# A two-layer hybrid encoder on one core: the gates' logarithm, decays and masks go behind k's convolutions

## The chip, the core and the metric

One NeuronCore of a Trainium2 chip. The metric is the device time of one execution in microseconds (us). The engines are TensorE (PE in the profile), VectorE (DVE), ScalarE (ACT), GpSimd (POOL) and SyncE (SP), each with an instruction stream of its own in a fixed order; they meet only at semaphores. A wait of one instruction therefore holds up everything behind it on its engine.

## The reference

Two pre-norm residual layers over 256 tokens of width 1024, float32 throughout. Each layer projects the normalised input by one weight matrix into eleven parts and runs two token mixers side by side: a gated DeltaNet in both directions (q, k, v through a short convolution and SiLU; 8 heads of 128) and a differential softmax attention (8 heads, 64 wide score halves). What the change touches is the gates of the DeltaNet:

```python
proj = h @ w_in[l]                       # 1024 x 10272
q_a, k_a, v_a, ab_a, z_a, q_b, k_b, v_b, z_b, gate_a, gate_b = split(proj)
qkv = silu(short_conv(concat(q_a, k_a, v_a), conv_w)); q, k = l2norm(q), l2norm(k)
beta = sigmoid(ab[:2])
g = -exp(a_log) * softplus(ab[2:] + dt_bias)          # ab: (4, heads, tokens)
g = cumsum(g)                                         # per chunk
decay = where(lower, exp(g[:, None] - g[None, :]), 0) # per head
L = where(strict, (k * beta) @ k.T * decay, 0); T = inv(I + L)
...                                                   # u, w, state recurrence, both directions
lam = exp(sum(lp[0] * lp[1])) - exp(sum(lp[2] * lp[3])) + lambda_init   # the attention's mixing weight
```

## The kernel before

**Weights.** Every projection streams its weights as tiles of 256 input rows by 512 columns. SP's queue loads `raw` (three buffers), ScalarE rounds it to `hi` (CAST, L308), VectorE forms `lo` = raw - hi (L310), and TensorE multiplies hi by the input's high part, lo by the high part, and hi by the low part. hi and lo have two buffers each, so the cast of a tile starts when TensorE has left the tile two before. Four tiles, kp 0 to 3, make one projection of 512 columns. A few casts are put on VectorE instead (`turned`): q group 1's tile 3, and tiles 0 and 1 of the second qk projection.

**Names.** Tiles carry the layer, the group and the tile in their names: `hi_q011` is layer 0, q group 1, kp 1; `hi_qk0003` is layer 0, qk part 00, kp 3. In the profile the numbers are left out (`hi_q`, `hi_qk`).

**One layer, in program order around the change.** First half of v for the attention; convolutions of k (two groups: projection `pf_k`, then ScalarE `cvk` and tanh `thk`, VectorE the taps, TensorE's transposes `ctk`, ScalarE's sums of squares `sqj` into `ssk`); second half of v (`vb1`); then

- `log_decays` (from L726): from the k sums of squares `kss` the norm `nrm` (a power on POOL, L730) and their logarithm; the softplus of the gates, `Ln` of `e_`/`ev` (both lie in one tile `ge`, which the logarithm reads together with kss, 128x80, L732); `glog`, TensorE's cumulative sums `grps`, their copy `grow`, which POOL's queue writes to DRAM (`gdr`), TensorE's transposes `gcps`, `ngc`, `E_` and `nE`, and the exponents' biases `lnc`.
- `conv("q", …, 0)` (`pf_q`) and `qk_part(0, 0)` (`pp_qk`, with a copy `stg`, rope on VectorE in tiles `r`, and TensorE's transposes `qkt`, copied to `qkT`).
- four times `decays(g, c)` and `weigh_k(g, c)`: a broadcast of gdr to all partitions into `B` (0.5 MB, POOL's queue), `kds`, two masks by `affine_select` on POOL, eight exponents (ScalarE, L791), then on VectorE `dsum` and `A` = kk * dsum with TensorE's gram matrix `kk`. The third and fourth broadcast are held behind the second mask (`cut`).
- `turn_blocks`, `conv("q", …, 1)`, `qk_part(0, 1)`, the convolutions of v, and later the gate parts (`zb`, `za`, …) among which the attention's scores `sc` run.

**What sets the order.** The code's order is a wish: a list scheduler places every instruction on its engine by what it expects to be ready, with the weights at high priority; `with behind(ins)` keeps an instruction from being placed before `ins`, and `mark[...]` holds such instructions (`mark["k01", 1][0]` is the cast of layer 0, k group 1, tile 1). What it gives out is the fixed order of each engine. Both layers are built by the same code.

## Time and profile before

| what | value |
|---|---|
| median of 3 runs | 751.38 us (750.87 to 751.71) |
| the profiled execution | 750.2 us, span 748.5 us |
| mean granted TensorE clock | 0.997 |
| busy: PE, DVE, ACT, POOL | 739.9, 588.6, 475.3, 143.5 us |
| TensorE in layer 0: both k groups, second half of v | 24.8 to 48.6, 48.7 to 60.2 us |
| then q group 0, qk part 00, q group 1, qk part 01 | 60.2 to 72.7, 72.7 to 87.0, 87.0 to 99.5, 99.5 to 112.6 us |
| the 32 exponents of layer 0 | 91.5 to 103.5 us |

A row of a timeline gives the start in us, the duration, the engine, the line, the operation with what it writes and reads, and how many of a kind follow one another; in brackets stands how long the engine was idle before it, and what ended that. Matrix multiplies are pipelined, so their cadence is read from one start to the next, not from the duration. Layer 1 repeats every row some 366 us later.

### The profile page before, as it was taken

The page shows a single profiled execution, that of the slowest core. Times are in us where ns is not written, and L with a number is a line of the kernel's source. Part 1 is how long each engine was busy: PE and PEld are TensorE (multiplying, and loading weights), DVE is VectorE, ACT ScalarE, POOL GpSimd, SP SyncE. Part 2 cuts the span into 40 slices and gives each one's busy share as a digit, 9 for nine tenths or more (in the row PEclk, how much of TensorE's full clock was granted, in tenths as well). Part 3 has the DMA queues.
Part 4 walks back from the last instruction along what each step waited for, and adds up shares of the span by engine and source line. Part 5 has one row for each costly group of instructions (what it writes and reads, how often), then busy time and mean ns, then how long its engine had stood idle before and what let it go on. Part 6 is the DMA issues. An engine that isn't in the chain of part 4 may idle for free.

```text
span 748.5 us, 13886 instructions
## 1 busy us (share of the span) xinstructions
PE 739.9 (99%) x5164; PEld 640.8 (86%) x5164; DVE 588.6 (79%) x1109; ACT 475.3 (64%) x1016; POOL 143.5 (19%) x221
## 2 busy tenths in 40 slices
PE   8999999999999999999999999999999999999996
PEld 6999889977888889888889889889778888998885
DVE  8686899999985965578667779999999679537782
ACT  6657675667876576645454677655687758566552
POOL 6000441112022450000000025202110425301000
PEclk9999999999999999999999999999999999999999
DMA  8752767776667462567674358768666747335641
GB/s 261 235 171 80 214 206 214 209 213 194 208 185 178 146 183 83 171 200 248 199 232 141 85 144 257 217 183 228 198 172 195 198 135 231 92 114 202 219 142 56
DMA packets 73733, 135.45 MB, mean 181 GB/s; under 512 B 12944, under 2 KB 13921, under 8 KB 73666
## 3 DMA queue, kind: packets, MB, share of 16 engines
q1 hardware_dynamic: 64750, 113.65, 50.0%
q0 software_dynamic: 7936, 19.35, 9.0%
q10 hardware_dynamic: 980, 1.58, 0.6%
q8 instruction: 40, 0.66, 0.4%
q14 instruction: 27, 0.22, 0.1%
HBM read 125.53 MB, written 9.01 MB: 180 GB/s over the span
## 4 chain that ended last, share of the span: by engine, by line
PE 97%; DMA 1%; issue 1%; DVE 0%; ACT 0%; SPq 0%; POOLq 0%; POOL 0%; DVEq 0%; ACTq 0%
PE pp_vb L369 4%; PE pp_qk L325 4%; PE pp_qk L324 4%; PE pp_qk L326 4%; PE sc L1033 2%; PE pp_o L369 2%; PE pp_za L325 2%; PE pf_v L385 2%; PE pf_k L385 2%; PE pf_v L389 2%; PE pp_gb L324 2%; PE pp_gb L325 2%; PE pp_zb L324 2%; PE pf_k L387 2%; PE pf_k L389 2%; PE pf_q L387 2%
## 5 line engine op out<-in xcount | busy, mean ns | idle before, releaser
L325 PE MATMUL pp_qk<-lo_qk,hT 128*128 128x512 f32 x128 | 50.7, 396 | 0.0
L326 PE MATMUL pp_qk<-hi_qk,hT 128*128 128x512 f32 x128 | 50.0, 390 | 0.0
L310 DVE TENSOR_TENSOR lo_qk<-raw_qk,hi_qk 128x1024 fp32r<-128x1024 f32 x32 | 39.5, 1234 | 9.6 <-ACT hi_qk L308 9.1
L324 PE MATMUL pp_qk<-hi_qk,hT 128*128 128x512 f32 x128 | 45.2, 394 | 0.0
L308 ACT CAST hi_qk<-raw_qk 128x1024 fp32r<-128x1024 f32 x28 | 29.4, 1049 | 23.6 <-PE pp_qk L326 11.8
L1043 ACT ACTIVATE es<-sc,mx 128x256 f32<-128x256 f32 x64 | 29.6, 474 | 19.6 <-DVE mx L1041 19.6
L310 DVE TENSOR_TENSOR lo_pb<-raw_pb,hi_pb 128x1024 fp32r<-128x1024 f32 x16 | 19.6, 1225 | 21.5 <-ACT hi_pb L308 21.2
L387 PE MATMUL pf_q<-hT,hi_q 128*128 128x256 f32 x128 | 36.2, 286 | 0.0
L385 PE MATMUL pf_q<-hT,hi_q 128*128 128x256 f32 x128 | 36.1, 286 | 0.0
L385 PE MATMUL pf_v<-hT,hi_v 128*128 128x256 f32 x128 | 35.8, 285 | 0.0
L385 PE MATMUL pf_k<-hT,hi_k 128*128 128x256 f32 x128 | 35.8, 285 | 0.0
L387 PE MATMUL pf_v<-hT,hi_v 128*128 128x256 f32 x128 | 35.8, 284 | 0.0
L387 PE MATMUL pf_k<-hT,hi_k 128*128 128x256 f32 x128 | 35.6, 283 | 0.0
L389 PE MATMUL pf_q<-hT,lo_q 128*128 128x256 f32 x128 | 34.8, 285 | 0.0
L389 PE MATMUL pf_v<-hT,lo_v 128*128 128x256 f32 x128 | 34.5, 287 | 0.0
L389 PE MATMUL pf_k<-hT,lo_k 128*128 128x256 f32 x128 | 34.3, 283 | 0.0
L670 DVE SCALAR_TENSOR_TENSOR cvq<-pf_q,cw,cvq 128x254 f32<-128x254 f32 (+1 forms) x64 | 29.9, 476 | 1.9 <-ACT cvq L666 1.4
L308 ACT CAST hi_pa<-raw_pa 128x1024 fp32r<-128x1024 f32 x16 | 16.9, 1054 | 22.2 <-PE pp_pa L326 16.0
L670 DVE SCALAR_TENSOR_TENSOR cvk<-pf_k,cw,cvk 128x254 f32<-128x254 f32 (+1 forms) x64 | 28.5, 478 | 2.1 <-ACT cvk L666 1.4
L670 DVE SCALAR_TENSOR_TENSOR cvv<-pf_v,cw,cvv 128x254 f32<-128x254 f32 (+1 forms) x64 | 29.7, 475 | 0.1
L325 PEld LDWEIGHTS pp_qk<-lo_qk,hT 128*128 128x128 f32 x128 | 24.0, 188 | 6.1 <-DVE lo_qk L310 1.3
L310 DVE TENSOR_TENSOR lo_pa<-raw_pa,hi_pa 128x1024 fp32r<-128x1024 f32 x16 | 19.6, 1224 | 11.2 <-ACT hi_pa L308 11.2
(409 smaller groups left out, 2541.2 us busy)
## 6 DMA issues: line engine op xcount, KB each, us to landing
raw_qk<-in_w_in_dram SPq DMA_DIRECT2D x32, 512.0 KB, 4.0
raw_k<-in_w_in_dram SPq DMA_DIRECT2D x16, 512.0 KB, 4.4
raw_q<-in_w_in_dram SPq DMA_DIRECT2D x16, 512.0 KB, 3.8
raw_v<-in_w_in_dram SPq DMA_DIRECT2D x16, 512.0 KB, 3.8
raw_zb<-in_w_in_dram SPq DMA_DIRECT2D x16, 512.0 KB, 3.9
raw_za<-in_w_in_dram SPq DMA_DIRECT2D x16, 512.0 KB, 3.8
raw_ga<-in_w_in_dram SPq DMA_DIRECT2D x16, 512.0 KB, 4.8
raw_pb<-in_w_pb_dram SPq DMA_DIRECT2D x16, 512.0 KB, 3.8
```

The lines of the kernel that those rows point to most:

```text
L308: high = (V.tensor_copy if kp in turned else S.copy)(hi[:, :, :n], raw[:, :, :n]).ins
L310: mark[nm, kp] = high, V.tensor_tensor(lo[:, :, :n], raw[:, :, :n], hi[:, :, :n].bitcast(F32), ALU.subtract).ins
L324: T.matmul(o, act[kt // 4][:, 0, kt % 4, ts_], hi, start=kt == 0, stop=False)
L325: T.matmul(o, act[kt // 4][:, 0, kt % 4, ts_], lo, start=False, stop=False)
L326: mark["proj"] = T.matmul(o, act[kt // 4][:, 1, kt % 4, ts_], hi, start=False, stop=kt == KT - 1).ins
L369: mark["proj"] = T.matmul(o, act[kt // 4][:, pa, kt % 4, ts_], ws[kt][1 + pw], start=kt == 0 and n_ == 0, stop=kt == KT - 1 and n_ == 2).ins
L385: T.matmul(o, hi[:, cs], act[kt // 4][:, 0, kt % 4, :], start=first, stop=False, skip_group_check=True)
L387: T.matmul(o, hi[:, cs], act[kt // 4][:, 1, kt % 4, :], start=False, stop=False, skip_group_check=True)
L389: T.matmul(o, lo[:, cs], act[kt // 4][:, 0, kt % 4, :], start=False, stop=done, skip_group_check=True)
L670: V.scalar_tensor_tensor(ca[:, o0:o1], acc[:, b, o0 + sft : o1 + sft], cw[:, j, cb : cb + 1], ca[:, o0:o1], ALU.mult, ALU.add)
L1033: mm = T.matmul(sp[n][:, qt * SEQ : (qt + 1) * SEQ], qkT[h // 4][rows, 0, h % 4, qt * P : (qt + 1) * P], qkT[h // 4][rows, 1, h % 4, :], s ...
L1043: S.activation(es[:, n, qt, :], spv[:, qt, :], AF.Exp, bias=mx[:, n, qt : qt + 1], accum_out=s_all[:, h, n, qt : qt + 1])
```

## The change

`log_decays` is split. `gates()` is called after the code of k's convolutions; its logarithm of the gates alone (128x64) is held behind the cast of k group 1, tile 0, and what follows from it (glog, grps, grow, gdr, gcps, ngc, E, nE) may be placed from there on. `lambdas()` takes the exponential of the attention's mixing weight, held behind the cast of k group 1, tile 1. `spread()` issues all four broadcasts in a row on POOL's queue, then the eight masks; the hold by `cut` goes. `log_decays` keeps the k norms, their logarithm (128x16) and the biases; `decays` keeps kds and the exponents.

```diff
         ls = small.tile([P, 2], F32, tag="ls", name=f"ls{l}")
         V.tensor_reduce(ls, lq, AX.X, ALU.add)
-        S.activation(ls, ls, AF.Exp)
         neglam = small.tile([P, 1], F32, tag="neglam", name=f"neglam{l}")
-        V.scalar_tensor_tensor(neglam, ls[:, 1:2], -lam0, ls[:, 0:1], ALU.add, ALU.subtract)
...
+        ngc = small.tile([P, 4, NH], F32, tag="ngc", name=f"ngc{l}")
...
         def log_decays():
...
-            S.activation(e_, e_, AF.Ln)
-            V.scalar_tensor_tensor(ev, a_, 0.0, ev, ALU.max, ALU.add)
-
+            S.activation(kss, kss, AF.Ln)
             for d in range(2):
                 V.scalar_tensor_tensor(lnc[:, d], ev[:, :, d * 8 : d * 8 + 8], -1.0, kss,
                                        ALU.mult, ALU.subtract)
+            V.tensor_tensor(lnc.rearrange("p d c h -> p (d c) h"), lnc.rearrange("p d c h -> p (d c) h"),
+                            ngc, ALU.add)
+
+        def lambdas():
+            with behind(mark[f"k{l}1", 1][0]):
+                S.activation(ls, ls, AF.Exp)
+            V.scalar_tensor_tensor(neglam, ls[:, 1:2], -lam0, ls[:, 0:1], ALU.add, ALU.subtract)
+
+        def gates():
+            with behind(mark[f"k{l}1", 0][0]):
+                S.activation(ev, ev, AF.Ln)
+            V.scalar_tensor_tensor(ev, a_, 0.0, ev, ALU.max, ALU.add)
             glog = small.tile([P, NM, 16], F32, tag="glog", name=f"glog{l}")
...
-        def decays(g, c, after=None):
+        def spread():
+            for g in range(2):
+                for c in range(NM):
+                    hs4 = slice(4 * g, 4 * g + 4)
+                    G.dma_start(out=B[:, c, hs4].rearrange("p h d i -> p (h d i)"),
+                                in_=gdr[c, hs4].rearrange("h d i -> (h d i)").partition_broadcast(P))
+            for g in range(2):
+                for c in range(NM):
+                    dec = B[:, c, 4 * g : 4 * g + 4].rearrange("p h d i -> p d h i")
+                    for d in range(2):
+                        sg = 1 - 2 * d
+                        G.affine_select(
+                            out=dec[:, d], in_=dec[:, d], compare_op=ALU.is_ge, fill=BIG,
+                            base=0, pattern=[[0, 4], [sg, P]], channel_multiplier=-sg)
+
+        def decays(g, c):
...
-            with behind(after):
-                G.dma_start(out=B[:, c, hs4].rearrange("p h d i -> p (h d i)"),
-                            in_=gdr[c, hs4].rearrange("h d i -> (h d i)").partition_broadcast(P))
...
-                mark["cut"] = G.affine_select(
...
         conv("k", C_KA, 0, 1)
+        gates()
         for _ in proj_by_tile(hT, wl, C_VB + 512, evac_v(1), f"vb{l}1", places2, spare=range(4),
...
+        lambdas()
+        spread()
         log_decays()
...
-        cut = mark["cut"]
         decays(0, 1)
...
-        decays(1, 0, cut)
+        decays(1, 0)
...
-        decays(1, 1, cut)
+        decays(1, 1)
```

Three places of the order in layer 0 matter for the prediction; layer 1 has the same rows with its own numbers. First ScalarE. Before, from the cast of q group 1's first tile on (`hi_q010`), `E_` being the exponential of ngc and `thq`, `cvq` the convolution's tanh and first tap:

```order
L308 CAST hi_q010_1196<-raw_q010_1198 128x1024
L676 ACTIVATE thq000_961<-cvq001_964 128x256
L757 ACTIVATE E_0_364<-ngc0_828 128x32
L586 COPY stg0000_1063<-pp_qk0000_989 128x512
L676 ACTIVATE thq002_978<-cvq002_972 128x256
L666 ACTIVATE cvq003_981<-pf_q001_834,cw0_294 128x256
L308 CAST hi_q011_1226<-raw_q011_1228 128x1024
L586 COPY stg0001_1076<-pp_qk0001_990 128x512
L308 CAST hi_q012_1256<-raw_q012_1258 128x1024
L599 ACTIVATE qkT0_0_307<-qkt0000_1070 128x4x128
L791 ACTIVATE B0_366<-B0_366,lnc0_362 128x128 x4
```

Now, from the cast of the last tile of qk part 00 on (the exponents are the rows of L805):

```order
L308 CAST hi_qk0003_1074<-raw_qk0003_1076 128x1024
L805 ACTIVATE B0_365<-B0_365,lnc0_360 128x128
L674 ACTIVATE thq000_990<-cvq001_993 128x256
L805 ACTIVATE B0_365<-B0_365,lnc0_360 128x128 x7
L308 CAST hi_q010_1197<-raw_q010_1199 128x1024
L805 ACTIVATE B0_365<-B0_365,lnc0_360 128x128 x3
L674 ACTIVATE thq002_1007<-cvq002_1001 128x256
L805 ACTIVATE B0_365<-B0_365,lnc0_360 128x128 x5
L664 ACTIVATE cvq003_1010<-pf_q001_863,cw0_294 128x256
L805 ACTIVATE B0_365<-B0_365,lnc0_360 128x128 x2
L586 COPY stg0000_1092<-pp_qk0000_1018 128x512
L805 ACTIVATE B0_365<-B0_365,lnc0_360 128x128
```

The next row is the cast of `hi_q011`, and twelve more exponents stand before that of `hi_q012`. All 32 were behind the last ScalarE cast of q group 1; 31 of them are ahead of it now.

VectorE, q group 1's last three tiles. Before:

```order
L310 TENSOR_TENSOR lo_q011_1227<-raw_q011_1228,hi_q011_1226 128x1024
L591 TENSOR_TENSOR r40001_1078<-stg0001_1076,sincos_284 128x128
L670 SCALAR_TENSOR_TENSOR cvq003_981<-pf_q001_834,cw0_294,cvq003_981 128x255
L592 TENSOR_TENSOR r40001_1078<-stg0001_1076,sincos_284 128x128
L670 SCALAR_TENSOR_TENSOR cvq003_981<-pf_q001_834,cw0_294,cvq003_981 128x254
L593 TENSOR_TENSOR stg0001_1076<-r40001_1078 128x8x8
L594 TENSOR_TENSOR stg0001_1076<-r40001_1078 128x8x8
L310 TENSOR_TENSOR lo_q012_1257<-raw_q012_1258,hi_q012_1256 128x1024
L308 CAST hi_q013_1286<-raw_q013_1288 128x1024
```

Now:

```order
L310 TENSOR_TENSOR lo_q011_1228<-raw_q011_1229,hi_q011_1227 128x1024
L812 TENSOR_TENSOR A0_364<-kk001_1146,dsum001_1144 128x512
L668 SCALAR_TENSOR_TENSOR cvq003_1010<-pf_q001_863,cw0_294,cvq003_1010 128x254
L591 TENSOR_TENSOR r40001_1107<-stg0001_1105,sincos_284 128x128
L592 TENSOR_TENSOR r40001_1107<-stg0001_1105,sincos_284 128x128
L811 TENSOR_TENSOR dsum010_1161<-B0_365 128x512
L593 TENSOR_TENSOR stg0001_1105<-r40001_1107 128x8x8
L594 TENSOR_TENSOR stg0001_1105<-r40001_1107 128x8x8
L812 TENSOR_TENSOR A0_364<-kk010_1163,dsum010_1161 128x512
L308 CAST hi_q013_1287<-raw_q013_1289 128x1024
L310 TENSOR_TENSOR lo_q012_1258<-raw_q012_1259,hi_q012_1257 128x1024
```

The dsum and A steps have come in, and the VectorE cast of tile 3 (`hi_q013`) stands ahead of tile 2's lo (`lo_q012`), where it stood behind it.

TensorE, at the second block of scores, in the gate projection zb. Before:

```order
L326 MATMUL pp_zb001_2022<-hi_zb003_2077,hT0_1_127 128x512
L1033 MATMUL sc011_2121<-qkT0_0_307 128x256
L1033 MATMUL sc010_2120<-qkT0_0_307 128x256
L1033 MATMUL sc011_2121<-qkT0_0_307 128x256
L1033 MATMUL sc010_2120<-qkT0_0_307 128x256
L324 MATMUL pp_zb010_2164<-hi_zb010_2166,hT0_0_126 128x512
```

Now:

```order
L326 MATMUL pp_zb001_2023<-hi_zb003_2078,hT0_1_127 128x512
L1047 MATMUL sc011_2122<-qkT0_0_307 128x256
L597 MATMUL qkt0111_2006<-ident_81,stg0111_1999 128x128 x4
L1047 MATMUL sc010_2121<-qkT0_0_307 128x256
L1047 MATMUL sc011_2122<-qkT0_0_307 128x256
L1047 MATMUL sc010_2121<-qkT0_0_307 128x256
L324 MATMUL pp_zb010_2165<-hi_zb010_2167,hT0_0_126 128x512
```

Four transposes qkt, which stood some ten rows ahead, have come between the first score multiply and the other three. Each of these rows is two instructions in the profile.

More of the change, by code (lines that the diff above doesn't have):

```diff
@@ L754, in log_decays @@
                 T.transpose(gc_ps[:, dc * 8 : dc * 8 + 8], grow[:, dc, :], ident[:8, :8])
-            ngc = small.tile([P, 4, NH], F32, tag="ngc", name=f"ngc{l}")
             V.tensor_scalar(ngc, gc_ps[:, :32].rearrange("p (c h) -> p c h", c=4), -1.0, None, ALU.mult)
@@ L758, in log_decays @@
             V.tensor_scalar(nE, E_, -1.0, None, ALU.mult)
-            V.tensor_tensor(lnc.rearrange("p d c h -> p (d c) h"), lnc.rearrange("p d c h -> p (d c) h"),
-                            ngc, ALU.add)
         A = big.tile([P, 2, NM, 4, P], F32, tag="A", name=f"A{l}")
@@ L784, in decays @@
             for d in range(2):
-                sg = 1 - 2 * d
-                mark["cut"] = G.affine_select(
-                    out=dec[:, d], in_=dec[:, d], compare_op=ALU.is_ge, fill=BIG,
-                    base=0, pattern=[[0, 4], [sg, P]], channel_multiplier=-sg).ins
                 for j4 in range(4):
```

## The prediction

> **What bounds the kernel now.** I read the head of the page first, then the chain that ended last, then TensorE's waits, and only then the stretches around the change.
>
> ```profile
> span 748.5 us, 13886 instructions
> PE 739.9 (99%) x5164; PEld 640.8 (86%) x5164; DVE 588.6 (79%) x1109; ACT 475.3 (64%) x1016; POOL 143.5 (19%) x221
> PE 97%; DMA 1%; issue 1%; DVE 0%; ACT 0%; SPq 0%; POOLq 0%; POOL 0%; DVEq 0%; ACTq 0%
> PE idle L410 <- DVE ones L407: 1.1, 1, 1.1
> PE pp_vb L454 <- ACT hT L234: 0.4, 1, 0.4
> PE pp_vb L454 <- DVE hT L238: 0.3, 1, 0.3
> ```
>
> TensorE is busy 99% of the span and is 97% of the chain; the last three rows are all its waits, 1.8 us (line, releaser, total, times, longest), and all lie at a layer's start, far from this change. The change removes no matrix multiply, so what it can win is only small hesitations of TensorE that the wait view does not list. What it can lose is open: any weight tile that arrives late stops TensorE.
>
> Where it acts is the stretch of q's convolutions and the first qk projection, 66 to 105 us in layer 0 and about 366 us later again in layer 1.
>
> ```profile
> 81.00:87.00 6.00, 6.00 (x38) 5.01 (x36) 5.31 (x14) 2.74 (x7) 2.02 (x4) 1.00 0.61 155
> 87.00:93.00 6.00, 6.00 (x53) 6.00 (x52) 5.42 (x13) 4.37 (x11) 3.57 (x6) 1.00 0.90 294
> 93.00:99.00 6.00, 6.00 (x52) 6.00 (x52) 5.48 (x7) 5.36 (x18) 3.27 (x7) 1.00 0.93 311
> ```
>
> Columns: stretch, length, then busy time of PE, PEld, DVE, ACT and POOL, granted clock, DMA share, GB/s. TensorE is full at clock 1.00 and VectorE at 5.3 to 5.5 of 6; ScalarE has 2.74 of 6 before 87 and 5.36 after 93. The 32 exponents of the decays are what fills it after 93. Where exactly they stand among the weight casts is the question of this prediction.
>
> ```profile
> 86.22 0.42 ACT L676 ACTIVATE thq<-cvq 128x256 f32<-128x256 f32 x1
> 86.54 0.47 ACT L666 ACTIVATE cvq<-pf_q,cw 128x256 f32<-128x256 f32 x1
> 86.90 1.04 ACT L308 CAST hi_q<-raw_q 128x1024 fp32r<-128x1024 f32 x1
> 87.83 0.60 ACT L586 COPY stg<-pp_qk 128x512 f32<-128x512 f32 x1
> 97.85 2.45 ACT L791 ACTIVATE B<-B,lnc 128x128 f32<-128x128 f32 x8 [0.62 <-POOL B L786]
> 88.29 1.22 DVE L310 TENSOR_TENSOR lo_q<-raw_q,hi_q 128x1024 fp32r<-128x1024 f32 x1
> 93.38 1.47 DVE L308 CAST hi_q<-raw_q 128x1024 fp32r<-128x1024 f32 x1 [0.92 <-PE pf_q L387]
> 97.56 0.80 DVE L308 CAST hi_qk<-raw_qk 128x1024 fp32r<-128x1024 f32 x1
> ```
>
> A weight tile goes raw (DMA), hi (a cast, mostly on ScalarE), lo (raw minus hi on VectorE, 1.22 us), TensorE. hi and lo have two buffers each, so a cast starts only when TensorE has left the tile two before. Now the second cast of q1 (86.90) follows short work, its lo ends at 89.51 and TensorE reads it first at 90.22 (row below): 0.7 us of slack, and that is all the chain has. The exponents come late, where the fourth q1 tile and the first two of the next projection are cast on VectorE instead (93.38), so no weight waits behind them.
>
> **The change, part by part.** I write R for the time at which TensorE leaves the second tile of the first qk projection, which releases the ScalarE cast of the fourth.
>
> ```profile
> 86.22 1.05 PE L772 MATMUL kk<-kq 128*128 128x128 f32 x8
> 87.03 0.36 PE L385 MATMUL pf_q<-hT,hi_q 128*128 128x256 f32 x1
> 89.87 0.60 PE L597 MATMUL qkt<-ident,stg 128*128 128x128 f32 x4
> 90.22 0.36 PE L389 MATMUL pf_q<-hT,lo_q 128*128 128x256 f32 x1
> 106.77 0.62 PE L324 MATMUL pp_qk<-hi_qk,hT 128*128 128x512 f32 x2
> 109.49 0.61 PE L324 MATMUL pp_qk<-hi_qk,hT 128*128 128x512 f32 x2
> 112.62 0.38 PE L385 MATMUL pf_v<-hT,hi_v 128*128 128x256 f32 x1
> ```
>
> 1. *The exponents among q1's casts (ScalarE).* In the new order eight exponents and a tanh stand between the cast of the last qk tile and that of q1's first, and eleven exponents with a tanh, a cvq and a stg copy between q1's first and second. By the starts in the rows a cast takes 0.93 (86.90 to 87.83), tanh 0.32, cvq 0.36; neighbours overlap by about 0.1, so a stg copy takes some 0.48 of its 0.60 and eight exponents 2.36 of their 2.45, 0.295 each. ScalarE then starts the second q1 cast at R + 0.2 (release) + 0.93 + 2.36 + 0.32 + 0.93 + 3.25 + 0.32 + 0.36 + 0.48 = R + 9.2. It ends 1.04 later; lo follows at once or after the rope steps of the stg copy that now stand ahead of it on VectorE (0.5 later), and takes 1.22: R + 11.4 to R + 12.0. TensorE wants it after two qk tiles (2.72 each, 106.77 to 109.49), q1's first tile (24 steps of 0.12: 23 stand between 87.03 and 89.87), the kk block now ahead of it (86.22 to 87.03 and the switch, 0.9), four hi rows (0.48) and qkt (0.35): R + 10.1 to 10.3. So it waits 1.1 to 1.8 us; I take 1.4. This holds if each exponent finds its data, which the POOL rows below bear out.
>
> 2. *q1's third tile (VectorE).* Its lo now stands behind the VectorE cast of the fourth tile, in the order before ahead of it. That cast waits for TensorE to leave the second tile, then takes 1.47 (93.38), then lo 1.22, 2.7 us after the release, where TensorE needs it after kk 0.9, qkt 0.35 and four hi rows 0.48, that is 1.73 after: 0.95 late, less if the cast takes the 0.8 us it took at 97.56. I take 0.7 (0 to 0.95). Terms 1 and 2 come in both layers, since the order is the same in both.
>
> 3. *A score block cut in two (TensorE).*
>
> ```profile
> 165.09 1.14 PE L1033 MATMUL sc<-qkT 64*128 64x256 f32 x8
> ```
>
> Eight score instructions of half height, alternating between the two halves, take 1.14 us, 0.28 a pair. If the halves of a pair run side by side, the lone ones that the cut leaves on each side cost a pair's time each, about 0.4 us with the switch; if not, only the switch of 0.1. 0 to 0.5, I take 0.4.
>
> 4. *Two table loads more per layer, around k's convolutions (ScalarE).*
>
> ```profile
> L732 ACT ACT_TABLE_LOAD  x2: 1283/1283/1283, 73.8 to 439.7; - x2
> L732 ACT ACTIVATE ge<-ge x2: 270/270/270, 75.1 to 441.0; 128x80 f32<-128x80 f32 x2
> 36.50 0.48 ACT L666 ACTIVATE cvk<-pf_k,cw 128x256 f32<-128x256 f32 x1 [1.25 <-PE pf_k L389]
> 39.92 1.05 ACT L308 CAST hi_k<-raw_k 128x1024 fp32r<-128x1024 f32 x1 [0.88 <-PE pf_k L387]
> 41.19 1.22 DVE L310 TENSOR_TENSOR lo_k<-raw_k,hi_k 128x1024 fp32r<-128x1024 f32 x1
> 43.20 0.28 PE L389 MATMUL pf_k<-hT,lo_k 128*128 128x256 f32 x1
> 402.29 0.47 ACT L666 ACTIVATE cvk<-pf_k,cw 128x256 f32<-128x256 f32 x1 [1.19 <-PE pf_k L389]
> 405.77 1.05 ACT L308 CAST hi_k<-raw_k 128x1024 fp32r<-128x1024 f32 x1 [1.83 <-PE pf_k L387]
> ```
>
> 2 x 1.28 plus at most 0.27 for each of the two short functions behind them. In layer 0 they fill the idle 1.25 ahead of 36.50 and the 0.88 ahead of the cast at 39.92, which comes 0.5 to 0.9 later; lo_k ended at 42.41 and was read at 43.20, so 0.79 covers it but for 0.1 at worst. In layer 1 the idle 1.19 and 1.83 of the last two rows cover it. I take 0 (0 to 0.3 a layer); if the cover goes, each tenth is a tenth of the time. The Trainium skill (ScalarE: Activation LUTs, "What ACT_TABLE_LOAD costs") puts a drain of about 1380 ns on top of each load, 2.66 us in all: by it the cast would be 2.8 us later still and TensorE would stall some 2.6 us here. The trace does not show that drain: the first load starts at 73.8 and the logarithm behind it at 75.1, so the row's 1.28 decides.
>
> 5. *What goes from the q stage.* The logarithm there shrinks from 128x80 to 128x16 (0.27 us) between its two loads, which stay; glog, grow, ngc, E and nE leave VectorE and ScalarE ahead of q1, under 2 us of off-path work. 0. The grps, gcps and four kk blocks are moved on TensorE, the same in number and in switches: 0, but R, 78.2 before (grps follows it), comes behind grps (0.97), gcps (0.4) and two kk now, at about 81.3. With the exponents done earlier, A and the blocks behind it come sooner; the hesitations in the tile from 109.49 to 112.62, 3.13 against 2.72, may go. 0 to 0.4, I take 0.2 off.
>
> 6. *Broadcasts and masks (POOL and its queue).*
>
> ```profile
> 72.66 0.63 PE L324 MATMUL pp_qk<-hi_qk,hT 128*128 128x512 f32 x2
> 78.22 1.04 PE L745 MATMUL grps<-tri,glog 128*8 128x128 f32 x8
> 89.43 0.34 POOL L783 TENSOR_TENSOR kds<-B,lnc 128x4 f32<-128x4 f32 x1 [4.58 <-DMA B<-gdr]
> L786 POOL TENSOR_SCALAR_AFFINE_SELECT B<-B x8: 627/862/1536, 89.7 to 101.0; 128x512 f32<-128x512 f32 x8
> DMA to landing us min/median/max: 5.6/6.7/7.5
> raw_q<-in_w_in_dram SPq DMA_DIRECT2D x1, 512.0 KB, 7.5
> raw_q<-in_w_in_dram SPq DMA_DIRECT2D x16, 512.0 KB, 3.8
> ```
>
> The grps block now stands 44 steps of 0.12 ahead of q0's end (72.66), so at about 67.3, 11 us ahead of its old place. The first broadcast was used 11.2 us behind it (78.22 to 89.43), so the first is to be had at 78.5, and the others, at 5.6 to 7.5 us to landing and more when four share the engines, by 85. Eight masks of 0.86 are done by 87, the last two 1.7 us behind the last landing. ScalarE reaches the first exponents at 82.4 and the ninth, which needs the third broadcast, at 86 (from R = 81.3). So they are ready: 0, with 0 to 1.4 us as the upper bound if the third is late. SP's queue keeps its order. Its loads took 7.5 us beside broadcasts against 3.8 in the middle case, and still came in time (the cast at 93.38 waited 0.92 us for TensorE, not for its load); the broadcasts only collide with other loads now.
>
> Sum per layer: 1.4 + 0.7 + 0.4 + 0 - 0.2 = 2.3 us, twice 4.6. The profiled execution took 750.2 us, its span 748.5, 1.2 under the median of the runs, 751.38; the difference is added to the median: **756.0 us**. With each term at its ends the forecast goes from 2 x 0.7 to 2 x 3.5: 752.8 to 758.4.
>
> **The rivals.** 0.2% is 1.5 us, about what a measurement here can tell from no change; all chances are counted by it.
>
> *The stall is absorbed* (same). If ScalarE's chain is shorter than I add up, or TensorE reaches q1 a microsecond later than I place it, the 0.7 us of slack holds and only the cut block is left, or not even that: 750.9 to 752.5. For it: a shift of 1.5 us in either term is enough, and I add up ten durations. Against: 19 exponents of 0.295 are 5.6 us set before a cast that had 0.7 to spare. 25%.
>
> *Faster.* The mechanism is the early end of the decays: A is done before the next projection, and TensorE loses its hesitations there and at the block's start. It is worth 0.4 us in each of the few places, at most 1.7 us in both layers, so 749.7; it decides only if terms 1 to 3 are all nought. 5%.
>
> *The four broadcasts crowd the weights* (slower still). Their 2 MB in one go against a load of 0.5 MB per 2.72 us: at the 311 GB/s of the row at 93, an even split leaves the weights 155 of the 193 they need, and over some 13 us they fall behind by 0.5 MB, about 1.6 us at that rate, against about 1 us of slack. With the third broadcast late too it adds 1 to 2 us a layer: 758 to 760. The Trainium skill (DMA: Bandwidth & Descriptors, "Queues, rings and completion order") has each engine alternate between queues packet by packet, which is the even split; the 7.5 us above agrees with it. Against: two pairs of broadcasts ran nearly back to back before and cost nothing. 10%.
>
> *The table loads stop k's convolutions* (slower too). If a load holds ScalarE a microsecond longer than its row, the cast of k's third tile comes 2 us later in layer 0 and 0.8 - 0.9 - 2 leaves TensorE 2.1 us short: 758.1. Against: the logarithm's start, right behind its load. 3%.
>
> **How the numbers follow.** Forecast (752.9 to 758.4) 57%, crowding 10%, table loads 3%, same 25%, faster 5%. Slower is 70%. The range runs from 751.0, which leaves out the faster case and about half of the same, to 759.6, which leaves out the end of the crowding. The likeliest case's own range is 752.9 to 758.4.
>
> **What would show it.** Step 1: TensorE rows waiting for ScalarE's hi_q or VectorE's lo_q at about 91 to 93 us (457 to 459), the second q1 cast with 11 exponents ahead. Step 2: a second wait at 95 to 98, on lo_q. Step 3: the second score block at about 1.5 us with qkt inside, not 1.07. Step 4: no wait on lo_k near 43. Step 6: the masks done by 87, POOL not named in ScalarE's waits. The prediction is wrong if q1's tiles follow at 2.88 plus kk and qkt with no wait, or if the long wait stands at k's convolutions instead.

## The result, and the profile after

| | before | after |
|---|---|---|
| median of 4 runs | 751.12 us (750.83 to 751.71) | 758.96 us (758.79 to 760.65) |
| ratio | | 1.0108, 95% interval 1.0091 to 1.0126 |
| span of the profiled execution | 748.5 us | 757.0 us |

The change made the kernel 7.8 us slower; the forecast was 756.0. One execution of the kernel before, beside e1 to e4, took 820.42 us at a mean granted clock of 0.85; it is in no ratio and no spread below. The same lines of the page as before:

```profile
span 757.0 us, 13901 instructions
PE 742.7 (98%) x5164; PEld 641.7 (85%) x5164; DVE 587.5 (78%) x1109; ACT 481.8 (64%) x1022; POOL 142.2 (19%) x221
PE 90%; ACT 3%; DVE 3%; DMA 2%; issue 2%; POOL 0%; POOLq 0%; DVEq 0%; SPq 0%; ACTq 0%
```

No engine has notably more work. What is new is in the chain, where ScalarE, VectorE and the DMA queues now hold 8%, and in TensorE's waits:

```profile
PE pf_q L385 <- ACT stg L586: 2.7, 2, 1.4
PE pp_qk L325 <- DVE lo_qk L310: 1.5, 3, 0.7
PE pf_q L389 <- DVE lo_q L310: 0.8, 1, 0.8
PE pf_q L385 <- ACT hi_q L308: 0.2, 1, 0.2
```

None of these four was there before, and all lie in the first qk projection and in q group 1. The stretches of layer 0 that the prediction showed, now:

```profile
81.00:87.00 6.00, 5.11 (x22) 3.60 (x21) 5.57 (x10) 4.46 (x11) 6.00 (x9) 1.00 0.75 272
87.00:93.00 6.00, 4.64 (x32) 4.08 (x31) 4.88 (x10) 6.00 (x18) 0.30 (x2) 1.00 0.55 174
93.00:99.00 6.00, 6.00 (x53) 5.93 (x52) 6.00 (x14) 6.00 (x19) 0.00 (x0) 1.00 0.33 91
```

ScalarE is full from 87 to 99, where q1's second and third casts stand. TensorE is short of 6.00 in the first half of that stretch and in the 6 us before it. To see where the time went, I compared the start of every projection on TensorE in the two traces, and, inside a projection, each step from one matrix multiply to the next with its usual step:

| place | layer 0 | layer 1 | what the steps show |
|---|---|---|---|
| q group 0 and first qk projection | +1.5 | +1.5 | waits of 0.85 and 0.36 us on lo_qk (layer 1: 0.80, and 0.23 for q1's first tile) |
| q group 1 and second qk projection | +1.7 | +2.6 | 1.5 in the middle of q1's first tile, 0.3 at the lo of its third; in layer 1 also 0.9 at the start of its first; 0.5 less at the end |
| from there to the layer's end | +0.8 | +0.8 | the score block cut in two |

With 0.25 us less at the start, these make the 8.5 us between the spans, up to rounding. The waits named in a row do not add up to all of it; the rest lies in smaller steps, which I have not followed. Now the rows. The long wait, on ScalarE and TensorE, layer 0 and in the last row layer 1:

```profile
83.89 0.42 ACT L674 ACTIVATE thq<-cvq 128x256 f32<-128x256 f32 x1 [0.96 <-DVE cvq L668]
...
86.26 1.03 ACT L308 CAST hi_q<-raw_q 128x1024 fp32r<-128x1024 f32 x1
...
90.80 0.56 ACT L586 COPY stg<-pp_qk 128x512 f32<-128x512 f32 x1
...
91.57 1.03 ACT L308 CAST hi_q<-raw_q 128x1024 fp32r<-128x1024 f32 x1
91.41 0.38 PE L385 MATMUL pf_q<-hT,hi_q 128*128 128x256 f32 x1 [1.36 <-ACT stg L586]
462.11 0.39 PE L385 MATMUL pf_q<-hT,hi_q 128*128 128x256 f32 x1 [1.35 <-ACT stg L586]
```

The step at 91.41 is the thirteenth of q1's first tile, the first that writes q1's second accumulator. Its weights and activations were read before; what it waits for is the accumulator's PSUM bank, which the stg copy at 90.80 sets free by reading the finished qk product out, and that copy stands behind ten exponents since the cast at 86.26. The cast at 91.57 is that of q1's second tile, 5.3 us behind the first with eleven exponents between. It comes late too, as VectorE and TensorE show:

```profile
93.40 1.22 DVE L310 TENSOR_TENSOR lo_q<-raw_q,hi_q 128x1024 fp32r<-128x1024 f32 x1
94.67 0.39 PE L389 MATMUL pf_q<-hT,lo_q 128*128 128x256 f32 x1
```

This lo ends at 94.62 and is read at 94.67, with no slack. Without the 1.36 us at the bank TensorE would have been there at 93.3 and waited for the lo instead, by an estimate from these rows 1.3 us: one group of exponents makes two things late, and only the first of them shows as a wait. Layer 1 has the same pair (lo ends at 465.31, read at 465.38).

In the kernel before, both had time to spare. The same copy and the first read of the second tile's lo there:

```profile
85.74 0.59 ACT L586 COPY stg<-pp_qk 128x512 f32<-128x512 f32 x1 [2.02 <-PE pp_qk L326]
90.90 0.28 PE L389 MATMUL pf_q<-hT,lo_q 128*128 128x256 f32 x1
```

The copy ended at 86.33 and the thirteenth step came at 88.55, 2.2 us later. The lo ended at 89.51 and was first read at 90.90, 1.4 us later: a tile has 24 steps, so the row at 90.22 from which the prediction took 0.7 us is the last step of q1's first tile and reads that tile's lo.

q1's third tile on VectorE and TensorE, now:

```profile
98.00 1.22 DVE L310 TENSOR_TENSOR lo_q<-raw_q,hi_q 128x1024 fp32r<-128x1024 f32 x1
99.27 0.39 PE L389 MATMUL pf_q<-hT,lo_q 128*128 128x256 f32 x1
```

The lo ends at 99.22, and the step that reads it comes 0.41 us behind the one before it (98.86) instead of 0.12. Layer 1 has the same 0.3 at 469.97. The first qk projection, third tile, layer 0; the first row is of the kernel before:

```profile
75.61 1.06 ACT L308 CAST hi_qk<-raw_qk 128x1024 fp32r<-128x1024 f32 x1 [0.20 <-PE pp_qk L326]
...
77.52 1.28 ACT L674 ACT_TABLE_LOAD   x1 [0.77 <-DVE cvq L668]
79.50 1.04 ACT L308 CAST hi_qk<-raw_qk 128x1024 fp32r<-128x1024 f32 x1
79.27 0.90 DVE L679 SCALAR_TENSOR_TENSOR kq<-thq,cvq 128x256 f32<-128x256 f32 x1 [1.72 <-ACT thq L674]
80.99 1.62 DVE L310 TENSOR_TENSOR lo_qk<-raw_qk,hi_qk 128x1024 fp32r<-128x1024 f32 x1
82.67 0.50 PE L325 MATMUL pp_qk<-lo_qk,hT 128*128 128x512 f32 x1 [0.69 <-DVE lo_qk L310]
```

The cast stands behind a table load and a tanh that wait for VectorE's taps; before, it stood ahead of them (75.61). And VectorE's steps are stretched: kq takes 0.90 and lo 1.62, against 0.42 and 1.22. In layer 1 the third tile is in time. There the fourth tile's lo is late, which stands behind five taps on VectorE (451.51 to 453.59) and takes 1.68 us, and TensorE waits 0.8 us for it; and the load of q1's first tile is late as well (the last two rows are of the DMA view: KB, and us to landing, of that load now and of the same load before):

```profile
453.59 1.68 DVE L310 TENSOR_TENSOR lo_qk<-raw_qk,hi_qk 128x1024 fp32r<-128x1024 f32 x1
456.94 1.05 ACT L308 CAST hi_q<-raw_q 128x1024 fp32r<-128x1024 f32 x1 [1.46 <-DMA raw_q<-in_w_in_dram]
459.30 0.39 PE L389 MATMUL pf_q<-hT,lo_q 128*128 128x256 f32 x1 [0.76 <-DVE lo_q L310]
raw_q<-in_w_in_dram SPq DMA_DIRECT2D x1, 512.0 KB, 10.5
raw_q<-in_w_in_dram SPq DMA_DIRECT2D x1, 512.0 KB, 3.7
```

Last the cut block of scores, with the four transposes inside:

```profile
175.20 0.70 PE L1047 MATMUL sc<-qkT 64*128 64x256 f32 x2
175.82 0.66 PE L597 MATMUL qkt<-ident,stg 128*128 128x128 f32 x4
176.41 1.13 PE L1047 MATMUL sc<-qkT 64*128 64x256 f32 x6
177.47 0.73 PE L324 MATMUL pp_zb<-hi_zb,hT 128*128 128x512 f32 x2
```

2.27 us from 175.20 to 177.47. Before, the whole block took 1.06 and the transposes inside the projection 0.44, so the cut costs 0.77.

### The profile page after: what moved, and what is told of

It is laid out like the page before. It is cut to its first block, busy times and chain, and to the rows that moved or that the text cites. A ratio compares the mean times of both kernels' runs of the same rounds, so it can differ in the third digit from the quotient of the medians.

```text
span 757.0 us, 13901 instructions
## 1 busy us (share of the span) xinstructions
PE 742.7 (98%) x5164; PEld 641.7 (85%) x5164; DVE 587.5 (78%) x1109; ACT 481.8 (64%) x1022; POOL 142.2 (19%) x221
## 4 chain that ended last, share of the span: by engine, by line
PE 90%; ACT 3%; DVE 3%; DMA 2%; issue 2%; POOL 0%; POOLq 0%; DVEq 0%; SPq 0%; ACTq 0%
PE pp_vb L369 4%; PE pp_qk L325 3%; PE pp_qk L326 3%; PE pp_qk L324 3%; PE sc L1047 2%; PE pp_o L369 2%; PE pp_zb L324 2%; PE pf_k L385 2%; PE pf_v L389 2%; PE pp_gb L325 2%; PE pp_za L325 2%; PE pp_gb L324 2%; PE pf_v L385 2%; PE pp_za L324 2%; PE pf_k L389 2%; PE pf_k L387 2%
```

## The experiments

Theory: the early gates let the exponents, and in the first qk projection a table load with a tanh, come ahead of weight casts on ScalarE; TensorE waits for those casts and for the stg copy among them. Rival: the four broadcasts and eight masks in a row crowd the DMA engines and VectorE. Each kernel was timed in five rounds beside the kernel before on the same chip; ratios are to that kernel, and 0.1% is 0.75 us. The kernel as changed stands at 1.0108.

**e1, the score block whole.**

```diff
-                    with behind(None if qt or not n else after), tc.high_priority(offset=HP):
+                    with behind(None if qt or not n else after), \
+                         behind(mark["qkt"] if h == 1 and n and not qt else None), tc.high_priority(offset=HP):
```

(`mark["qkt"]` is the last transpose of the qk projections.)

> The changed kernel with one edit: the second score block's first multiply is held behind the transposes qkt that had come between its multiplies, so the block runs whole; the order differs from the changed kernel in that row alone, once per layer. The trace of the changed kernel has the cut block with qkt inside at 2.27 us, against 1.06 for a whole block and 0.44 for qkt inside a projection, so the cut costs 0.8 us a layer. Theory (the time lies in TensorE's stream: cut block and late casts): 1.6 us less than the changed kernel, 757.3. Rival (the cut is only a place where a wait shows that would come later anyway, the score chain being set by VectorE and ScalarE): no gain, 758.9.

Measured 756.90 us, ratio 1.0088 (1.0075 to 1.0100): 0.2% less than as changed, 1.5 us, as the rows say, though the two intervals overlap. The trace is clearer: the block takes 1.06 us again (174.97 to 176.03), and from v's convolution to the layer's end TensorE falls back by 0.1 us instead of 0.8. The block was a loss by itself.

**e2, the exponents behind q1's casts.** The four `decays` and `weigh_k` calls go behind `conv("q", C_QA, 1, 1)`, and

```diff
-                    S.activation(dec[:, d, j4, :], dec[:, d, j4, :], AF.Exp,
-                                 bias=lnc[:, d, c, h : h + 1])
+                    with behind(mark[f"q{l}1", 2][0]):
+                        S.activation(dec[:, d, j4, :], dec[:, d, j4, :], AF.Exp,
+                                     bias=lnc[:, d, c, h : h + 1])
```

> The changed kernel with the code of the decays put behind that of q group 1's convolution and the 32 exponents held behind the cast of q1's third tile (kp 2). Gates, broadcasts, masks and table loads stay as in the changed kernel; the score block comes out whole again. Theory (exponents among ScalarE's weight casts stop TensorE in q1): the waits in q1 go, 1.7 and 2.6 us, and the cut block's 0.8 twice, while the waits on lo_qk in the first qk projection, 1.2 to 1.5 us a layer, stay, since the cast of its third tile still stands behind a table load and a tanh: 752.8 to 754.2. Rival (four broadcasts and eight masks in a row crowd DMA and VectorE): q1 stays slow, 757 or more.

Measured 753.66 us, ratio 1.0045 (1.0028 to 1.0061): more than half of the loss is gone, with gates, broadcasts, masks and loads as in the change. The wait on the stg copy in q1 is gone in its trace; what is left stands in the first qk projection, as expected, and at q1's first tile in layer 1, which waited 3.17 us for its raw load on ScalarE:

```profile
PE pp_qk L325 <- DVE lo_qk L310: 1.6, 3, 1.2
78.80 1.49 DVE L679 SCALAR_TENSOR_TENSOR kq<-thq,cvq 128x256 f32<-128x256 f32 x1 [1.73 <-ACT thq L674]
```

**e3, broadcasts and masks as before.** `spread()` goes; each `decays` has its broadcast and masks again, and `cut` its hold.

```diff
-        spread()
...
-        decays(1, 0)
+        decays(1, 0, cut)
```

> The changed kernel without the broadcasts and masks in a row: each decay issues its own broadcast and masks again, the later two held by cut as before; gates and table loads stay early. The exponents still stand among the weight casts, 16 of them ahead of q1's first cast and the first 4 ahead of the fourth qk tile's. Theory (order of ScalarE): still slow, 757 to 762, with longer waits at q1's first tile. Rival (broadcasts and masks in a row): back to 751 to 753.

Measured 758.89 us, ratio 1.0103 (1.0090 to 1.0116): the whole loss is still there. TensorE now waits longest on lo in q1:

```profile
PE pf_q L389 <- DVE lo_q L310: 3.1, 3, 1.5
```

So the loss does not need the row of broadcasts and masks. Since the exponents stand still earlier here than in the change, the run does not show that the row costs nothing.

**e4, the gates in their old place.** One logarithm again, and `gates()` called from `log_decays`; `spread()` behind it.

```diff
-        gates()
         for _ in proj_by_tile(hT, wl, C_VB + 512, evac_v(1), f"vb{l}1", places2, spare=range(4),
...
-            S.activation(kss, kss, AF.Ln)
+            S.activation(e_, e_, AF.Ln)
+            gates()
...
-            with behind(mark[f"k{l}1", 0][0]):
-                S.activation(ev, ev, AF.Ln)
```

> The changed kernel with the gates' part back in its old place behind the k norms, one logarithm for both; broadcasts and masks stay in a row, the table load for the mixing weight stays early. TensorE's, ScalarE's and VectorE's orders come out nearly as before the change, with the exponents behind q1's casts. Theory (the early gates let the exponents come among the casts, and that is the loss): 751 to 752. Rival (broadcasts and masks in a row): half or more of the loss stays, 755 to 759.

Measured 752.28 us, ratio 1.0013 (1.0004 to 1.0022). Seven of the eight microseconds come back; the early gates are the cause, through the order that they allow. The one that stays is, by its trace, the rival's, and it has a row: the fourth q1 tile's cast, which VectorE does, waited for its load, and the load took 10.5 us beside four broadcasts in a row.

```profile
95.34 0.76 DVE L308 CAST hi_q<-raw_q 128x1024 fp32r<-128x1024 f32 x1 [2.31 <-DMA raw_q<-in_w_in_dram]
```

**f1 and g1, the table loads behind the cast (on e2).**

```diff
-            S.activation(kss, kss, AF.Ln)
+            with behind(mark[f"qk{l}00", 2][0]):
+                S.activation(kss, kss, AF.Ln)
...
-        log_decays()
         conv("q", C_QA, 1, 0)
         qk_part(0, 0)
+        log_decays()
```

> On top of the kernel with the exponents late (e2): the code of the k norms is put behind that of the first qk projection and their logarithm is held behind the cast of its third tile (kp 2), so this cast no longer stands behind two table loads; TensorE's and POOL's orders are those of e2. In e2 TensorE still waited on lo_qk: 1.37 and 0.35 us in layer 0, 0.26, 0.36, 0.20 and 0.93 in layer 1. Theory A (the cast is late by its place on ScalarE): most of these 3.5 us go, 750.5 to 751.8. Theory B (POOL's masks, which run at 79 to 87 us, stretch VectorE's steps, kq 1.49 us instead of 0.42 and lo_qk 1.55 instead of 1.22): the masks stay where they are, so the waits stay for the most part, 752.8 to 754.

> The same kernel as f1 once more, for its spread: f1's executions went from 751.35 us (the profiled one, with 0.72 us of waits in layer 0's q1 and 1.4 in layer 1's, clock 1.00 throughout) to 756.63. Theory (TensorE's granted clock halves for some microseconds behind waits in q1, as the profiles of f3 at 90 to 94 and 458 to 464 us show it, in some executions and not in others): times from 751 to 757 again, and where the profile has a stretch below 1.00 near 88 to 96 or 456 to 466 its time is 1.5 to 3 us higher than 751.4 for each. Rival (weight loads beside the four broadcasts are late in some executions): a slow profile shows waits on DMA or on casts that wait for DMA, at clock 1.00.

Measured 754.36 us, ratio 1.0049 (1.0032 to 1.0066), and again 754.04, 1.0039 (1.0026 to 1.0053): by their medians no better than e2, so theory A's forecast of the time failed; but the fourteen executions go from 751.35 to 756.63. The profiled ones are among the lowest, 751.35 and 752.45. In them the waits of the first qk projection are gone from layer 0 and 0.3 in layer 1, although the masks run beside VectorE as before (lo_qk took 1.72 us): theory A holds for those waits. What is left there are 0.7 us in layer 0 and some 1 to 1.7 in layer 1 at q1's first two tiles, where the first cast waits for its load (0.7 to 2.5 us on ScalarE). Neither profiled execution shows why others of the same kernel take 3 to 5 us more.

**f2, the masks behind the last lo (on e2).**

```diff
+        def masks():
+            late = small.tile([P, 1], F32, tag="late", name=f"late{l}")
+            slow = G.tensor_copy(late, mark["lo", f"qk{l}00", 3][:, 0, 0:1].bitcast(F32)).ins
+            ...                                      # the eight masks, each behind(slow)
...
         qk_part(0, 0)
+        masks()
```

> On top of the kernel with the exponents late (e2): POOL first copies one column of the fourth qk tile's lo and only then runs the eight masks, so they start behind VectorE's last lo of that projection; ScalarE's order there, with the cast behind the loads, is that of e2. Theory A (place of the cast): 753 to 754 as e2. Theory B (masks stretch VectorE): kq back to 0.42 and lo_qk to 1.22, that is 1.4 us earlier, most of the waits in the first qk projection go, 751.3 to 752.5; the masks then run beside q1's lo steps, which may cost some tenths there, since the slack was 0.7.

Measured 755.18 us, ratio 1.0055 (1.0043 to 1.0067). The half of theory B on VectorE is shown, the forecast of the time is not. VectorE and POOL in layer 0:

```profile
79.69 0.42 DVE L680 SCALAR_TENSOR_TENSOR kq<-thq,cvq 128x256 f32<-128x256 f32 x1 [1.72 <-ACT thq L675]
80.99 1.23 DVE L311 TENSOR_TENSOR lo_qk<-raw_qk,hi_qk 128x1024 fp32r<-128x1024 f32 x1
91.19 1.67 DVE L311 TENSOR_TENSOR lo_q<-raw_q,hi_q 128x1024 fp32r<-128x1024 f32 x1
85.77 6.01 POOL L799 TENSOR_SCALAR_AFFINE_SELECT B<-B 128x512 f32<-128x512 f32 x8
```

With the masks out of the way kq is back at 0.42 and lo_qk at 1.23, and the wait of 1.37 us at the third qk tile is gone, with the cast where it was. But the masks now lie on q1, where lo_q takes 1.67 instead of 1.22 and TensorE waits 1.1 us in layer 0. In layer 1 it waits 2.1 at q1's first tile, whose cast stood idle 3.97 us for its load. The wait at the third qk tile took both, a cast made late by its place and a VectorE slowed by masks; either one alone is covered.

**f3, both edits.**

> Both edits on the kernel with the exponents late: logarithm of the k norms behind the cast of the third qk tile, masks behind the fourth tile's lo. Both theories: no waits left in the first qk projection, 750.5 to 751.8. If it stays above 752.5 there is a third cause, such as the masks beside q1's lo steps or the broadcasts in a row.

Measured 754.97 us, ratio 1.0060 (1.0048 to 1.0072), so there was a third cause. The waits in the first qk projection are gone in both layers, and 1.8 us in each stands at q1's first tile. The third cause is in its trace: that tile's cast waited for its weight load, which took 10.0 us in both layers. ScalarE in layer 0:

```profile
86.41 1.04 ACT L308 CAST hi_q<-raw_q 128x1024 fp32r<-128x1024 f32 x1 [2.24 <-DMA raw_q<-in_w_in_dram]
```

The lo behind it takes 1.25 us although masks run beside it, so neither they nor the moved table load make it late. Behind the wait the clock falls as well, as the last section shows.

**f4, the mixing weight's exponential alone, on the kernel before.**

```diff
-        S.activation(ls, ls, AF.Exp)
...
+            with behind(mark[f"k{l}1", 1][0]):
+                S.activation(ls, ls, AF.Exp)
```

> The kernel before with one part of the change: the exponential of the attention's mixing weight is held behind the cast of k group 1's second tile, with its table load; TensorE's and POOL's orders stay as before. My price in the prediction: a load of 1.28 us in ScalarE's idle time, nothing, 750.5 to 751.5. Rival (a load holds ScalarE 1.4 us longer than its row): the k cast late by up to 2 us, 752 to 753.5.

Measured 750.48 us, ratio 1.0000 (0.9991 to 1.0008). It cost nothing, but it does not test what I said: its trace has no table load at this exponential, since no logarithm stands ahead of it. The price of the loads is read from the changed kernel instead, at k's third tile (ScalarE, VectorE, TensorE):

```profile
38.83 1.28 ACT L740 ACT_TABLE_LOAD   x1
41.30 1.23 DVE L310 TENSOR_TENSOR lo_k<-raw_k,hi_k 128x1024 fp32r<-128x1024 f32 x1 [0.19 <-ACT hi_k L308]
42.94 0.28 PE L389 MATMUL pf_k<-hT,lo_k 128*128 128x256 f32 x1
```

The exponential behind the load starts at 40.12. lo_k ends at 42.53 and is read at 42.94, without a wait: 0.4 of the 0.79 us of cover is left.

**g2 and g3, small masks (on f1 and on e2).** These two kernels mask 2 of 128 columns and scale the decay rates to a thousandth, so they do not compute the reference; they are timed only.

```diff
-        V.tensor_scalar(nega, nega, -1.0, None, ALU.mult)
+        V.tensor_scalar(nega, nega, -0.001, None, ALU.mult)
...
-                            out=dec[:, d], in_=dec[:, d], compare_op=ALU.is_ge, fill=BIG,
-                            base=0, pattern=[[0, 4], [sg, P]], channel_multiplier=-sg)
+                            out=dec[:, d, :, 0:2], in_=dec[:, d, :, 0:2], compare_op=ALU.is_ge, fill=BIG,
+                            base=0, pattern=[[0, 4], [sg, 2]], channel_multiplier=-sg)
```

> f1 with masks that cover 2 of 128 columns, and with the decay rates scaled to a thousandth so that the exponents stay finite; the orders stay those of f1 but for the place of one short exponential (kds). Theory (masks stretch VectorE's steps, and the waits that come of it halve the clock now and then): the waits in q1 go, 750.3 to 751.5, and the executions lie within 2 us of each other. Rival (broadcasts crowd the loads): the spread to 756 stays.

> The kernel with the exponents late (e2), the cast of the third qk tile still behind two table loads, with masks of 2 columns and decay rates scaled as in g2. Theory B (masks stretch VectorE): kq at 0.42 and lo_qk at 1.22 us, the waits on lo_qk fall from 1.7 us in layer 0 to 0.4 or less, 751.0 to 752.0. Theory A (the place of the cast alone): the waits stay, 753 to 754.

g3 measured 752.88 us, ratio 1.0035 (1.0021 to 1.0049), g2 753.70, 1.0038 (1.0024 to 1.0052). In g3 kq and the third tile's lo took their bare time and the 1.37 us at the third qk tile are gone, with the cast behind its two loads: theory B, a second time. The total moved less than that (e2 is at 1.0045, and the intervals overlap). In g2 the waits did not go and the spread stayed (752.59 to 755.52): masks are not the last cause. ScalarE's row and TensorE's behind it, layer 1 of g2:

```profile
453.48 1.04 ACT L308 CAST hi_q<-raw_q 128x1024 fp32r<-128x1024 f32 x1 [3.30 <-DMA raw_q<-in_w_in_dram]
454.58 0.39 PE L385 MATMUL pf_q<-hT,hi_q 128*128 128x256 f32 x1 [1.78 <-ACT hi_q L308]
```

The weight load, 11.0 us beside four broadcasts, was late, and ScalarE stood idle until it landed.

The load of q1's first tile runs through all these kernels. Before, it took 4.4 us in layer 0 and 3.7 in layer 1. With early gates and the four broadcasts in a row (the change, e1, e2, f1 to f3, g1 to g3) it took 8.2 to 11.0; its cast waited 0.7 to 4.0 us for it in layer 1 of every one of them, and 0.7 to 2.6 in layer 0 of the f and g ones. With early gates and the broadcasts apart (e3) it took 5.4 and 7.0, and the cast did not wait for it. No kernel here has the exponents late and the broadcasts apart, so how much of the 0.45% that e2 keeps is the load's stays open.

**g4, the first term of the prediction by itself, on the kernel before.**

```diff
+                if nm[0] == "q" and nm[1:2] != "k" and nm[-1] == "1" and kp == 1:
+                    for _ in range(7):
+                        S.activation(hi[:, 0, :P], ident, AF.Exp)
                 with behind(act):
```

> The kernel before, with seven exponents more on ScalarE right ahead of the cast of q1's second tile, written into that tile's hi and then overwritten by the cast: 7 x 0.295 = 2.07 us, in both layers. This is the prediction's first term by itself, at a smaller dose. By the trace of before the slack is 0.7 us, so TensorE waits 1.36 us a layer: 753.3, range 752.5 to 754. If the clock halves behind such a wait it adds 1.5 to 3 us a layer in the executions where it happens: 755 to 759 in some of them. Rival (a late cast is caught up by the buffers): 751.

Measured 752.36 us, ratio 1.0022 (1.0012 to 1.0032), 1.6 us or 0.8 a layer; I expected 1.36, so only the sign is right: the late cast is not caught up. ScalarE and TensorE in layer 0:

```profile
87.08 2.04 ACT L309 ACTIVATE hi_q<-ident 128x128 fp32r<-128x128 f32 x6
91.63 0.39 PE L392 MATMUL pf_q<-hT,lo_q 128*128 128x256 f32 x1 [0.61 <-DVE lo_q L313]
```

The step is 0.77 us late (1.03 in layer 1). The delay was not smaller than I meant it to be: measured from q1's first step the second cast starts 2.7 us later than before, seven exponents and the stg copy that now stands ahead of it, and its lo ends 2.55 later. The slack was larger than the 0.7 that I had read: 1.39, and 0.44 by a second group of transposes that has come ahead of the read, leave 0.7 by an estimate from these rows. A weight cast delayed past its slack is paid for by TensorE, about one for one.

No version here beats the kernel before: f4 is level with it, and of those with the row of broadcasts e4, which has the gates in their old place, comes nearest, 0.1% behind.

## Why the prediction was right, and where not

The sign and the main mechanism were right, and the time lay in the range, near its upper end; the sum was short by 3.2 us of 7.8.

1. *Exponents among q1's casts.* Forecast 1.4 us a layer, measured 1.52 and 1.50, and R at 81.37 for 81.3. The size was right and the place was not: I let TensorE wait for lo in q1's second tile, and it waits one tile earlier, for the PSUM bank behind the stg copy, which I had only as an item of ScalarE's sum. That the size fits is partly luck. The cast started at 91.57, 1.0 us behind the R + 9.2 of the sum, since the tanh at 83.89 waited 0.96 us for VectorE; and TensorE came to q1 at 88.28, 1.5 us later than two tiles behind R, mostly by the waits on lo_qk. The sum had neither, and the two misses cancel. The 0.7 us of slack, on which the rival of the absorbed stall rests, was a misreading too: it was 1.4. e2 and e4 show that the exponents' place is the cause, g4 that a late cast is paid as well.
2. *q1's third tile.* Forecast 0.7, measured 0.3 in each layer, at just this lo. The VectorE cast took 0.68 us, not the 1.47 of the row that I took: that row had a mask beside it, and by 93 the masks were over.
3. *The cut block.* Forecast 0.4, measured 0.77, beyond my upper end of 0.5. The half-height steps at the cut cost more than I had allowed (0.62 us for the two ahead of it, 175.20 to 175.82), and I had counted one switch where there are two.
4. *Table loads at k's convolutions.* 0 was right. The drain that the Trainium skill adds (ScalarE: Activation LUTs, "What ACT_TABLE_LOAD costs") does not show here either: the exponential behind the load at 38.83 starts at 40.12, right at the load's end. By 2.66 us a load TensorE would have waited.
5. *The q stage.* This is the step that failed. I wrote that the logarithm there shrinks "between its two loads, which stay", and put 0; the loads stayed in number, but the cast of the third qk tile, ahead of the second load before, came behind it and a tanh. Together with masks on VectorE this made the third tile's lo 0.85 us late in layer 0 (f1 and f2 show that it took both). At the fourth tile, whose lo came to stand behind five taps on VectorE, it cost 0.36 in layer 0 and, with masks beside the lo, 0.8 in layer 1; for these two the cause is read from the rows, not tested. The order showed it, a few rows ahead of the piece that I quoted. The gain that I set at 0.2 was 0.5.
6. *Broadcasts.* 0 was right for the exponents, but for 0.29 us at the first of layer 1, and wrong for the weights there: 1.15 us at q1's first tile behind a load of 10.5 us. It is the rival that I gave 10%, at about half of its price, besides the forecast and not in its place. Where the exponents are late, as in f1 to g3, this load is the longest wait that is left. The Trainium skill's alternation by packets (DMA: Bandwidth & Descriptors, "Queues, rings and completion order") agrees with the 10.5 against 3.7.

That the stall would be absorbed, and that the change would be faster, the waits exclude; the table loads as a rival too.

## What to carry to other kernels

Where one engine feeds casts to a saturated TensorE, an early input for other work is no gift: a scheduler will place that work as soon as it can, ahead of casts and PSUM copies that have little slack, here 1.4 and 2.2 us. Read the new order over the whole stretch in which something moves, cast by cast and bank by bank, also where the instructions kept their number. And when durations are taken from a trace, ask what ran beside the row: the 1.47 us cast was a 0.68 us cast beside a mask.

## What the runs showed of the hardware

TensorE's granted clock can fall to half behind short waits. In f3, windows of 1 us in layer 0 (columns as above), and its steps:

```profile
87.00:88.00 1.00, 0.49 (x2) 0.30 (x2) 0.51 (x1) 1.00 (x3) 1.00 (x3) 1.00 0.15 55
88.00:89.00 1.00, 0.22 (x2) 0.21 (x2) 1.00 (x2) 1.00 (x3) 1.00 (x1) 1.00 0.02 8
90.00:91.00 1.00, 1.00 (x8) 1.00 (x7) 1.00 (x6) 0.05 (x1) 0.69 (x4) 0.53 0.78 174
91.00:92.00 1.00, 1.00 (x6) 1.00 (x6) 1.00 (x2) 0.00 (x0) 0.00 (x0) 0.50 0.79 307
...
90.10 0.42 PE L386 MATMUL pf_q<-hT,hi_q 128*128 128x256 f32 x1
90.31 0.42 PE L388 MATMUL pf_q<-hT,hi_q 128*128 128x256 f32 x1
```

Two waits of 0.7 and 0.8 us, 1.3 us apart, and then steps of 0.21 us instead of 0.12 for over 3 us. (At the very end of the span, where TensorE runs out of work, the clock falls to 0.50 in every trace here; that is not meant.) Added up over windows of 2 us, such a stretch loses 1.7 us (f2 in layer 1, f3 in each layer) or 3.4 (e1 and g2 in layer 1). These four profiled executions lie at or near the top of their kernels' times; of those without a stretch, f1, g1 and g3 lie at or near the bottom and e2 in the middle. The mean granted clock, which is on record for every execution, fits in part: in e2, f1, f3, g2 and g3 the slowest execution has 0.993 to 0.996 and the fastest 0.997 to 0.998, while in f2, e4 and g4 there is no such order. That makes it a likely reason why e2 and the kernels made from it spread over 2.5 to 5.5 us while the kernel before stays within 2.6; it is not shown. Nor do such waits always bring it on: the changed kernel and e3, with waits of 1.4 and 1.5 us, have no such stretch around q1. The Trainium skill (TensorE: Matmul & The Clock Gate) gives a rule by idle gaps of over about 3.4 us ("HAM oscillation — how this bites in real kernels"), which here no gap comes near, and tells of a kernel whose frequent short idles made the clock fall too ("A second HAM failure mode: psum-queue depth-cycling"); the runs agree with the second, and that page gives no number of short waits at which it begins.

POOL's masks slow VectorE's steps of two SBUF inputs (kq 0.42 to 1.49 us, lo 1.22 to 1.72), while the convolution's taps, which read a PSUM tile and one in SBUF, kept 0.99 us for two. Not every such step is slowed: in the changed kernel the lo at 84.62 kept 1.22 us beside two masks that took 2.40 us together, where two had taken 1.40 at 79.26. The Trainium skill (SBUF — State Buffer, "Who interferes with whom") has this rule, that such a VectorE step and a GpSimd instruction that reads SBUF exclude each other; f2 and g3 agree with it.
